# A step-wise softplus, another price for short VectorE instructions, and parameter fetches placed between weight loads

## Chip, cores and metric

The kernel runs on one core of a Trainium2 chip. The metric is the device time of one execution in microseconds (us), as the median over runs; lower is better.

## What is computed

The reference runs two two-layer models one after the other on 256 tokens of width 1024, in float32. A layer of the first kind (called a here) mixes four branches (a state-space scan, two softmax attentions, and an attention on the 64 best keys of an index) with gates and then has a gated feed-forward. A layer of the second kind (b) mixes four other branches (latent attention, spatial gating, gated linear attention, a delta rule), then has a cross attention and a feed-forward. What the change touches in it is softplus, which each kind uses on a few numbers per token:

```python
# layer a, mamba2_branch and fox_branch (log_sigmoid(x) = -softplus(-x))
dt = jax.nn.softplus(dt_raw.astype(jnp.float32) + dt_bias.astype(jnp.float32))   # [1, 256, 8]
log_f = jax.nn.log_sigmoid(f_logit.astype(jnp.float32) + f_bias)                 # [1, 256, 8]
...
# layer b: log_sigmoid of the 128 gate channels of the gated linear attention,
# softplus of 4 step sizes per token of the delta rule
```

and the small parameters of each layer (norm gains, biases, convolution taps, low-rank matrices), which are inputs in HBM.

## The kernel before

**Work.** Layers a0, a1, b0, b1 run in this order. The 256 tokens are two tiles of 128 partitions. All large products are TensorE matmuls on float32 data: each weight chunk (128 partitions x 1024 words, 512 KB) is loaded by one DMA into one of 4 `raw` slots, ScalarE (ACT) copies it rounded to fp32r ("hi", method `high`), VectorE (DVE) writes the remainder ("lo", method `low`), and three fp32r matmuls (hi x hi, hi x lo, lo x hi) make one float32 product (`mm3`). So each chunk costs one long ACT and one long DVE instruction, and TensorE (PE) can use it only after both. Up to 5 chunks are prepared ahead (`LOOK`).

**Order.** The whole program is laid out at build time: one stream of instructions for each engine, executed in order. The layout comes from a planner: a model of the engines' clocks (`Model`, with instruction prices from `Engine.cost`) is advanced as instructions are written down. The main line writes the large matmuls; after each group of them it calls `tick`. `tick` steps side work, which is held as Python generators: `spawn`ed ones, and four *lanes* that carry the branches. A lane is stepped from one `yield` to the next, at most once per tick, only if the model says that its last results are ready by PE's clock, and not while the model has DVE or ACT more than `BACKLOG` = 2750 ns ahead of PE (`behind`). `advance`, called by most ticks, writes `low` and `high` for the coming chunks. When the main line needs the result of a branch that is not finished, `drain` steps the lanes until it is. The plan is made twice; the second pass knows when each chunk falls due.

**Softplus.** `softplus` writes |x| and exp(-|x|) on ACT, then `log1p` writes 14 DVE instructions (an addition, a reciprocal, a series of odd powers in `scalar_tensor_tensor` steps), then one more on DVE. For n = 256 columns (lane C in layers b, `gla`) it yields three times on its way. For n = 32 (lane B in layers a, `small`) and n = 8 (lane B in layers b, `dn`, the delta rule) all of it is written without a yield, so it stands in one piece in DVE's stream. In `dn` two more short instructions stand before it and one behind.

**Prices.** For DVE `Engine.cost` takes (columns + 66)/0.96 ns, or (columns/2 + 66)/0.96 ns for a copy or tensor-scalar instruction outside PSUM, plus 61 ns for each per-partition scalar operand.

**Fetches.** All DMAs are issued by SyncE's queue (SP), in program order, by `Kern.dma`; SP waits in front of each for the buffer to be free. In the feed-forward of each layer but the last, after the first two blocks, `early` allocates and fetches what the next layer needs: constants when the kind changes (`load_consts`, `load_b`; a1 only), and its parameters (`params`): 3 DMAs for a layer a, 8 for a layer b, one behind the other.

Of the kernel before, what the change touches and what calls it, by code (L numbers as in the profile page):

```python
# [165 lines left out]
class Arena:  # L166
# [3 lines left out]
    def __init__(self, ap, words, name, aligned=False):  # L170
        self.ap, self.name, self.aligned = ap, name, aligned
        self.free_ = [(0, words, 0)]
        self.clock = 0
        self.live = {}
        self.pressure = None
# [127 lines left out]
def pair(k, tag):  # L303
    return Pair([Mat(k, 4, 256, tag) for _ in range(2)])
# [49 lines left out]
class Engine:  # L354
# [19 lines left out]
    def cost(self, fn, outs, ins, kw):  # L374
        if self.name == "PE":
            if fn == "transpose":
                return 109.0
            rows, m, n = ins[0].shape[0], ins[0].free_size(), ins[1].free_size()
            if ins[0].dtype == F32R:
                return max(m / 1.2, n / 2.4 + 12) + 1.5  # L380
            if rows <= 64 and m <= 64:
                return 68.0
            share = 0.67 if min(rows, m) <= 64 else 1.0
            return share * 2 * max(m / 1.2 + 1, n / 1.2 + 2)
        n = max(a.free_size() for a in outs[:1] + ins)
        psum = any("PSUM" in str(a.space) for a in ins + outs)
        ptr = sum(1 for a in ins if a.free_size() == 1) if n > 1 else 0
        if self.name == "ACT":
            return (94 if psum else 147) + n / 1.2 + 93 * (ptr + (len(outs) > 1))
        if self.name == "POOL":  # L390
            return 300 + 167 * n if kw.get("op") == OP.pow else 150 + 2.1 * n
        if fn in ("tensor_copy", "tensor_scalar", "memset") and not psum:
            return (n / 2 + 66) / 0.96 + 61 * ptr
        return (n + 66) / 0.96 + 61 * ptr + (1600 * n / 256 if fn == "reciprocal" else 0)


class Kern:
    def __init__(self, tc, dram, layers, tiles, due=None):
        self.tc, self.nc, self.dram, self.layers = tc, tc.nc, dram, layers
        self.due, self.used, self.gemm = due, {}, 0.0  # L400
        nc = self.nc
        self.model = Model()
        self.V, self.A, self.P, self.T = (Engine(e, n, self.model, due is None) for e, n in (
            (nc.vector, "DVE"), (nc.scalar, "ACT"), (nc.gpsimd, "POOL"), (nc.tensor, "PE")))
        wr = NPAIR * 2 * SLOT
        rt, ft, qt, raw, self.junk, banks = tiles
        self.R = Arena(rt[:, wr:], R_ACT, "R", True)
        self.F = Arena(ft, F_WORDS, "F")
        self.Q = Arena(qt, Q_WORDS, "Q")
        self.rawfree = deque(raw[:, i * SLOT:(i + 1) * SLOT] for i in range(NRAW))  # L410
        self.pairfree = deque((rt[:, (2 * i) * SLOT:(2 * i + 1) * SLOT], rt[:, (2 * i + 1) * SLOT:(2 * i + 2) * SLOT])
                              for i in range(NPAIR))
        self.banks = deque(banks)

        self.chunks = []
        self.index = {}
        for layer in layers:
            cbs = plan(layer)
            ch, _ = chunks_of(cbs)
            for name, p, off, nkt, c in ch:  # L420
                self.index[(layer, name, p)] = len(self.chunks)
                self.chunks.append((layer, off, nkt, c))
        self.i_dma = self.i_prep = self.i_done = self.i_cur = 0
        self.raws, self.pairs, self.half = {}, {}, deque()
        self.look = LOOK
        self.lanes = {}
        self.deferred = []
        self.ready, self.mark, self.active, self.pressed = {}, {}, [], 0
        self.keys, self.spawned = {}, 0
        self.gain0 = None  # L430
        self.R.pressure = self.F.pressure = self.Q.pressure = self.relieve


    def dma(self, out, in_):
        if self.due is not None:
            self.nc.sync.dma_start(out, in_)  # L436
        if "SB" in str(out.space):
            self.model.op("DMA", out.nbytes() / 400.0, 2900.0, [out], [])
# [53 lines left out]
    def load(self, most=NRAW):  # L492
        while self.rawfree and self.i_dma < len(self.chunks) and most:
            most -= 1
            layer, off, nkt, c = self.chunks[self.i_dma]
            raw = self.rawfree.popleft()
            src = self.dram["wts_%s%d" % layer][off:off + 128 * nkt * c].rearrange("(p f) -> p f", p=128)
            self.dma(raw[:, :nkt * c], src)
            self.raws[self.i_dma] = raw
            self.i_dma += 1  # L500

    def high(self):

# [327 lines left out]
    def log1p(self, e, out, n):  # L831

        f = self.F.alloc(3 * n, "l1p")
        a, b, c = f.a[:, :n], f.a[:, n:2 * n], f.a[:, 2 * n:3 * n]
        self.ts(a, e, 2.0, OP.add)
        self.V.reciprocal(b, a)
        self.tt(a, e, b, OP.mult)
        if n > 64:
            yield
        self.tt(b, a, a, OP.mult)  # L840
        self.ts(c, b, 1.0 / 17, OP.mult)
        for k in (15, 13, 11, 9, 7, 5, 3):
            if n > 64 and k in (13, 7):
                yield
            self.stt(c, c, 1.0 / k, b, OP.add, OP.mult)
        self.ts(a, a, 2.0, OP.mult)
        self.stt(out, c, 1.0, a, OP.add, OP.mult)
        f.free()

    def softplus(self, x, out, n):  # L850
        f = self.F.alloc(2 * n, "sp")
        a, b = f.a[:, :n], f.a[:, n:2 * n]
        self.act(a, x, AF.Abs)
        self.act(a, a, AF.Exp, scale=-1.0)
        yield from self.log1p(a, b, n)
        self.stt(out, x, 0.0, b, OP.max, OP.add)
        f.free()
# [833 lines left out]
    def layer_b(self, l, hT, nxt, pr, early):  # L1691
# [309 lines left out]
        def dn():  # L2001
# [4 lines left out]
                yield  # L2006
            self.tt(v2(x4), tokv[:, :, 16:20], dtb[:, None, :].to_broadcast([128, 2, 4]), OP.add)
            self.act(v2(be), tokv[:, :, 20:24], AF.Tanh, scale=0.5)
            self.ts(be, be, 1.0, OP.add, 0.5, OP.mult)
            yield from self.softplus(x4, x4, 8)  # L2010
            self.act(ge[:, 0:4], alog, AF.Exp)
# [575 lines left out]
def write(k, layers):  # L2587
    dram = k.dram
    F = k.F
    st = {}  # L2590

    def load_consts(kind):
        if st.get("kind") == kind:
            return
        if "cb" in st:
            st.pop("cb").free()
        st["kind"] = kind
        if kind == "a":
            cb = st["cb"] = F.alloc(NC_A, "ca")
            k.dma(cb.a[:, :NC_A], dram["const_a"])  # L2600
            k.amask, k.mmask, k.tri1 = cb.a[:, 0:384], cb.a[:, 384:768], cb.a[:, 768:1024]
            k.ropec, k.ropes = view(cb.a[:, 1024:1152], 2, 64), view(cb.a[:, 1152:1280], 2, 64)
            k.sel = cb.a[:, 1280:1297]
        else:
            k.load_b(st)

    k.startup(layers[0])
    load_consts(layers[0][0])
    pr = k.params(layers[0])
    hT = pair(k, "hT")  # L2610
    first = k.norm_steps(0, k.x[:, 0], pr["gain"].a, lambda: hT)
    for _ in range(3):
        k.scoped(next, first)
    k.high()
    k.low()
    k.spawn(first, "h0")
    k.flush("h0")

    def second(gain):
        yield from k.norm_steps(1, k.x[:, 1], gain.a, lambda: hT)  # L2620
        gain.free()
    k.spawn(second(pr.pop("gain")), "h1")
    for _ in range(2):
        k.high()
        k.low()
    for i, (kind, l) in enumerate(layers):
        last = i == len(layers) - 1
        nxt_h = {}

        def early(i=i, last=last, nxt_h=nxt_h):  # L2630
            if not last:
                load_consts(layers[i + 1][0])
                nxt_h["p"] = k.params(layers[i + 1])

        def nxt(t, f, i=i, last=last, nxt_h=nxt_h):
            if last:
                yield from k.finish(t, f)
                return
            if t == 0:
                nxt_h["h"] = pair(k, "hT")  # L2640
            yield from k.norm_steps(t, k.x[:, t], nxt_h["p"]["gain"].a, lambda: nxt_h["h"], f)
            if t == 1:
                nxt_h["p"].pop("gain").free()
        if kind == "a":
            k.ffn_a(l, k.layer_a(l, hT, pr), nxt, early)
        else:
            k.layer_b(l, hT, nxt, pr, early)
        if not last:
            k.drain(until=lambda: "h" in nxt_h)
            hT, pr = nxt_h["h"], nxt_h["p"]  # L2650
    k.flush()
    return k.used
# [91 lines left out]
```

## Time and profile before

| | us |
|---|---|
| median of 3 runs (2263.59 to 2268.12) | 2264.24 |
| the profiled execution | 2261.76 |
| its span, first to last instruction | 2259.9 |
| PE busy in the span | 2220.2 (98%) |
| PEld (weight loads, beside PE) busy | 1898.7 (84%) |
| DVE busy | 1535.9 (68%) |
| ACT busy | 1075.5 (48%) |
| POOL (GpSimd) busy | 300.4 (13%) |

A view of the profile is read as follows. Busy times say how much an engine worked, not whether it was waited for; the views of waits and of the order of instructions in time say that. [...] A time in brackets behind an instruction is the idle time of its engine just before it, with what ended it. Instructions of one form that follow one another closely are merged in one row of the order in time (x7: seven of them).

### The profile page before, as it was taken

Reading aid. Unit: us, or ns where it says so; the run is one execution under the profiler, and the core shown is the slowest. Engines: PE = TensorE matmul, PEld = TensorE weight load, DVE = VectorE, ACT = ScalarE, POOL = GpSimd, SP = SyncE. Lnnn points to the kernel's source line nnn. Section 1 sums busy time; section 2 is a strip of 40 time slices with the busy share of each in tenths; the row PEclk is TensorE's granted clock in tenths of the full one; section 3 lists DMA queues with packets and bytes.
Section 4 is the critical chain, followed back from the end, with each engine's and each line's share of the span. In section 5 each row is a group of like instructions: output and inputs, shape, how many; then the busy total and the mean of one; then the engine's idle time right before and its main releaser. Section 6 shows DMA issues by size and latency. Waiting matters only on the chain.

```text
span 2259.9 us, 36096 instructions
## 1 busy us (share of the span) xinstructions
PE 2220.2 (98%) x14196; PEld 1898.7 (84%) x14196; DVE 1535.9 (68%) x2487; ACT 1075.5 (48%) x1699; POOL 300.4 (13%) x266
## 2 busy tenths in 40 slices
PE   8999999999999999999998999999999999999998
PEld 6887788999788788899886788988988677898897
DVE  7887777556888776764777767465566776746554
ACT  4555545444454554543554345444445533545543
POOL 2102110000302120000134220000002432000000
PEclk9999999999999999999998999999999899999999
DMA  6444665655444566565433265456553434544563
GB/s 220 150 133 144 202 227 183 209 176 174 149 131 141 163 202 219 202 215 187 151 105 122 95 206 182 142 176 230 181 163 113 139 112 161 187 159 158 188 210 106
DMA packets 108950, 379.37 MB, mean 168 GB/s; under 512 B 12730, under 2 KB 13164, under 8 KB 108780
## 3 DMA queue, kind: packets, MB, share of 16 engines
q1 hardware_dynamic: 108780, 377.07, 51.0%
q8 instruction: 111, 1.82, 0.3%
q14 instruction: 59, 0.48, 0.1%
HBM read 375.97 MB, written 1.05 MB: 167 GB/s over the span
## 4 chain that ended last, share of the span: by engine, by line
PE 87%; DVE 6%; POOL 2%; issue 2%; ACT 1%; DMA 1%; SPq 0%; POOLq 0%; DVEq 0%; ACTq 0%
PE bank L364 87%; DVE ft L364 4%; DVE rt L364 2%; POOL ft L364 2%; ACT ft L364 1%; DMA raw<-in_wts_a 1%; ACT rt L364 0%; DMA ft<-in_positions 0%; DMA raw<-in_wts_b 0%; ACT junk L364 0%; DVE qt L364 0%; ACT L364 0%; SPq L436 0%; POOLq L2739 0%; POOLq L364 0%
## 5 line engine op out<-in xcount | busy, mean ns | idle before, releaser
L364 PE MATMUL bank<-rt 128*128 128x512 f32 (+3 forms) x10608 | 1975.5, 344 | 13.4 <-DVE rt L364 12.3
L364 PEld LDWEIGHTS bank<-rt 128*128 128x128 f32 x10608 | 1647.7, 190 | 248.0 <-DVE rt L364 18.8
L364 DVE TENSOR_TENSOR rt<-raw,rt 128x1024 fp32r<-128x1024 f32 (+2 forms) x692 | 842.2, 1242 | 266.3 <-ACT rt L364 265.5
L364 ACT ACTIVATE rt<-raw 128x1024 fp32r<-128x1024 f32 (+2 forms) x692 | 693.9, 1034 | 302.1 <-PE bank L364 144.5
L364 POOL TENSOR_TENSOR ft<-ft 128x512 f32<-128x512 f32 (+9 forms) x208 | 247.4, 1200 | 1816.7 <-DVE ft L364 1673.7
L364 PE MATMUL bank<-ft 64*64 64x64 f32 (+13 forms) x3540 | 330.9, 268 | 19.5 <-DVE ft L364 11.8
L364 PEld LDWEIGHTS bank<-ft 64*64 64x64 f32 (+7 forms) x3540 | 254.4, 148 | 102.9 <-issue 35.3
L364 ACT ACTIVATE ft<-bank 128x512 f32<-128x512 f32 (+5 forms) x256 | 135.3, 537 | 334.6 <-PE bank L364 297.8
L364 ACT ACTIVATE ft<-ft 128x128 f32<-128x128 f32 (+7 forms) x238 | 107.6, 463 | 244.0 <-DVE ft L364 228.1
L364 ACT ACTIVATE rt<-bank 128x512 fp32r<-128x512 f32 (+1 forms) x114 | 63.3, 560 | 132.0 <-PE bank L364 131.7
L364 DVE TENSOR_TENSOR ft<-ft 128x512 f32<-128x512 f32 (+5 forms) x122 | 69.2, 568 | 74.2 <-ACT ft L364 71.9
L364 DVE SCALAR_TENSOR_TENSOR ft<-ft 128x512 f32<-128x512 f32 (+5 forms) x211 | 94.3, 467 | 35.1 <-ACT junk L364 16.2
L364 DVE TENSOR_TENSOR ft<-bank,ft 128x512 f32<-128x512 f32 (+8 forms) x160 | 74.1, 491 | 44.6 <-PE bank L364 31.0
L364 DVE SCALAR_TENSOR_TENSOR ft<-ft,bank 128x512 f32<-128x512 f32 (+1 forms) x110 | 70.8, 644 | 35.3 <-PE bank L364 25.7
L364 DVE TENSOR_TENSOR ft<-ft,bank 64x512 f32<-64x512 f32 (+3 forms) x88 | 56.6, 644 | 43.0 <-PE bank L364 39.8
L364 DVE SCALAR_TENSOR_TENSOR ft<-bank,ft 128x256 f32<-128x256 f32 (+5 forms) x124 | 60.4, 509 | 24.7 <-PE bank L364 9.3
L364 DVE TENSOR_SCALAR ft<-ft 128x256 f32<-128x256 f32 (+7 forms) x230 | 58.4, 297 | 26.0 <-ACT ft L364 10.4
L364 DVE COPY ft<-bank 128x384 f32<-128x384 f32 (+5 forms) x96 | 49.3, 541 | 28.5 <-PE bank L364 25.4
L364 ACT ACTIVATE junk<-ft 128x512 bf16<-128x512 f32 (+1 forms) x46 | 27.2, 592 | 64.4 <-DVE ft L364 61.6
L364 POOL TENSOR_SCALAR qt<-qt,ft 64x256 fp32r<-64x256 f32 (+1 forms) x32 | 37.2, 1164 | 131.5 <-PE bank L364 130.6
L364 DVE SCALAR_TENSOR_TENSOR rt<-bank,rt 128x512 fp32r<-128x512 f32 (+1 forms) x72 | 43.3, 612 | 16.5 <-ACT rt L364 16.2
L364 ACT ACTIVATE rt<-ft 128x512 fp32r<-128x512 f32 x46 | 29.0, 630 | 48.7 <-DVE ft L364 47.0
(37 smaller groups left out, 311.2 us busy)
## 6 DMA issues: line engine op xcount, KB each, us to landing
raw<-in_wts_a SPq DMA_DIRECT2D x340, 512.0 KB, 4.2
raw<-in_wts_b SPq DMA_DIRECT2D x312, 512.0 KB, 4.3
raw<-in_wts_b SPq DMA_DIRECT2D x24, 256.0 KB, 2.6
ft<-in_b_gate SPq DMA_DIRECT2D x16, 256.0 KB, 4.5
raw<-in_wts_b SPq DMA_DIRECT2D x8, 440.0 KB, 4.2
raw<-in_wts_a SPq DMA_DIRECT2D x8, 340.0 KB, 4.6
ft<-in_mem SPq DMA_DIRECT2D x4, 512.0 KB, 7.3
ft<-in_x SPq DMA_DIRECT2D x2, 512.0 KB, 3.7
```

What stands on the lines that cost most here:

```text
L364: r = None if self.dry else f(*args, **kw)
```

## The change

Three edits. First, a DVE instruction of at most 64 columns, other than a reciprocal, is priced at 185 ns plus 61 ns for each per-partition scalar. Second, `log1p` yields at its three places whatever n is, `softplus` yields between its ACT part and `log1p`, and `dn` yields between its tanh on ACT and the DVE instruction that reads it. No instruction is added or left out by these yields. Third, while `early` runs `params`, `dma` only notes the fetches; after each weight chunk that `load` issues, one noted fetch is issued. `fetch_all` issues what is left when the next layer's norm begins. Buffers are allocated where they were.

```diff
@@ Engine.cost (DVE)
+        if n <= 64 and fn != "reciprocal":
+            return 185.0 + 61 * ptr
         if fn in ("tensor_copy", "tensor_scalar", "memset") and not psum:
             return (n / 2 + 66) / 0.96 + 61 * ptr
         return (n + 66) / 0.96 + 61 * ptr + (1600 * n / 256 if fn == "reciprocal" else 0)
@@ Kern.__init__
+        self.pend, self.holding = deque(), False
@@ Kern.dma
     def dma(self, out, in_):
+        if self.holding:
+            self.pend.append((out, in_))
+            return
         if self.due is not None:
             self.nc.sync.dma_start(out, in_)
@@ Kern.load (in its loop over free raw slots)
             self.i_dma += 1
+            if self.pend:
+                self.dma(*self.pend.popleft())
+
+    def fetch_all(self):
+        while self.pend:
+            self.dma(*self.pend.popleft())
@@ log1p
         self.tt(a, e, b, OP.mult)
-        if n > 64:
-            yield
+        yield
         self.tt(b, a, a, OP.mult)
         self.ts(c, b, 1.0 / 17, OP.mult)
         for k in (15, 13, 11, 9, 7, 5, 3):
-            if n > 64 and k in (13, 7):
+            if k in (13, 7):
                 yield
             self.stt(c, c, 1.0 / k, b, OP.add, OP.mult)
@@ softplus
         self.act(a, a, AF.Exp, scale=-1.0)
+        yield
         yield from self.log1p(a, b, n)
@@ dn (layer_b)
             self.act(v2(be), tokv[:, :, 20:24], AF.Tanh, scale=0.5)
+            yield
             self.ts(be, be, 1.0, OP.add, 0.5, OP.mult)
             yield from self.softplus(x4, x4, 8)
@@ write: early
                 load_consts(layers[i + 1][0])
+                k.holding = True
                 nxt_h["p"] = k.params(layers[i + 1])
+                k.holding = False
@@ write: nxt
             if t == 0:
+                k.fetch_all()
                 nxt_h["h"] = pair(k, "hT")
```

## Rows read from the trace of the kernel before

**Rows 1.** The page: TensorE's busy time, and its granted clock in 40 slices.

```profile
PE 2220.2 (98%) x14196; PEld 1898.7 (84%) x14196; DVE 1535.9 (68%) x2487; ACT 1075.5 (48%) x1699; POOL 300.4 (13%) x266
...
PEclk9999999999999999999998999999999899999999
```

**Rows 2.** Busy time by stretch: stretch, length, engines (instructions), clock, DMA share, GB/s.

```profile
0.00:50.00 50.00, 38.74 (x182) 31.19 (x183) 36.27 (x75) 23.76 (x35) 12.50 (x16) 1.00 0.65 227
...
1170.00:1240.00 70.00, 59.55 (x551) 49.36 (x551) 51.89 (x106) 34.07 (x72) 36.41 (x33) 0.88 0.39 125
1240.00:1750.00 510.00, 509.98 (x3417) 441.06 (x3418) 322.91 (x451) 239.48 (x363) 53.07 (x50) 1.00 0.50 165
1750.00:1800.00 50.00, 44.84 (x291) 34.03 (x290) 34.52 (x74) 28.39 (x57) 22.16 (x20) 0.86 0.45 137
...
2250.00:2260.00 10.00, 3.03 (x14) 2.18 (x12) 2.45 (x5) 1.45 (x3) 0.55 (x1) 0.78 0.14 52
```

**Rows 3.** Waits of TensorE over the span: releaser, us in total, times, longest.

```profile
PE bank L364 <- DVE rt L364: 12.3, 12, 4.9
PE bank L364 <- DVE ft L364: 11.8, 6, 7.5
PE bank L364 <- POOL ft L364: 7.5, 9, 2.3
```

**Rows 4.** Order in time at the start of layer b0: start, us, instruction, [idle before].

```profile
1187.35 1.31 DVE L364 TENSOR_SCALAR ft<-ft 128x8 f32<-128x8 f32 x2 [1.46 <-ACT ft L364]
...
1189.54 1.37 DVE L364 SCALAR_TENSOR_TENSOR ft<-ft 128x8 f32<-128x8 f32 x7
...
1191.58 2.23 DVE L364 TENSOR_TENSOR rt<-raw,rt 128x512 fp32r<-128x512 f32 x2
...
1192.32 0.80 PE L364 MATMUL bank<-rt 128*128 128x256 f32 x2 [4.91 <-DVE rt L364]
...
1194.85 4.70 PE L364 MATMUL bank<-ft 128*4 128x128 f32 x20
```

**Rows 5.** Busy time in stretches of 2 us, layers b0 and b1.

```profile
1190.00:1192.00 2.00, 0.00 (x0) 0.00 (x0) 1.69 (x10) 0.88 (x1) 0.27 (x1) 0.64 0.00 0
...
1774.00:1776.00 2.00, 2.00 (x12) 1.78 (x11) 1.88 (x4) 0.00 (x0) 0.00 (x0) 0.56 0.38 70
```

**Rows 6.** Order in time at the start of layer b1.

```profile
1771.15 0.30 PE L364 MATMUL bank<-ft 128*128 128x128 f32 x1 [0.86 <-DVE ft L364]
1771.81 4.30 PE L364 MATMUL bank<-ft 128*128 128x128 f32 x25 [0.36 <-DVE ft L364]
...
1790.54 0.42 DVE L364 SCALAR_TENSOR_TENSOR rt<-bank,rt 128x256 fp32r<-128x256 f32 x1
...
1791.01 0.99 PE L364 MATMUL bank<-rt 128*128 128x512 f32 x2 [2.01 <-DVE rt L364]
```

**Rows 7.** Order in time at the starts of layers a0 and a1.

```profile
42.07 0.66 PE L364 MATMUL bank<-ft 128*128 128x128 f32 x4 [1.28 <-POOL ft L364]
...
590.58 1.28 DVE L364 TENSOR_TENSOR ft<-bank,ft 128x512 f32<-128x512 f32 x2
...
594.17 0.66 PE L364 MATMUL bank<-ft 128*128 128x128 f32 x4 [2.28 <-POOL ft L364]
```

**Rows 8.** DVE instructions by form: busy us, mean ns, idle before.

```profile
L364 DVE SCALAR_TENSOR_TENSOR ft<-ft 128x32 f32<-128x32 f32 x25 | 4.8, 192 | 0.9
...
L364 DVE SCALAR_TENSOR_TENSOR ft<-ft 128x8 f32<-128x8 f32 x20 | 3.3, 167 | 0.8
```

**Rows 9.** Order in time around the fetches for layer b0, in layer a1.

```profile
948.45 0.17 DVE L364 CAST ft<-ft 128x2 f32<-128x2 int32 x1 [5.67 <-DMA ft<-in_positions]
...
953.92 0.33 SPq L436 DMA_DIRECT2D ft<-in_sgw  x1
...
955.71 34.30 SPq L436 DMA_DIRECT2D raw<-in_wts_a  x16
...
960.67 0.98 PE L364 MATMUL bank<-rt 128*128 128x256 f32 x6 [0.67 <-DVE rt L364]
```

## Prediction

> **What bounds the kernel now.** I read the page first. PE is busy for 2220.2 of 2259.9 us [rows 1], so 39.7 us is all that waiting costs, and no edit here takes a matmul away. Next come the stretches: from 1240 to 1750 us PE lacks 0.02 us [rows 2], and it is as full in most other places. The 39.7 us sit in a few: 11.3 in the first 50 us, 10.5 at the start of b0 (1170 to 1240), 5.2 at the start of b1 (1750 to 1800), 7.0 at the very end [rows 2], the rest mainly at the start of a1 and in the feed-forward of a1. The first load and the last store make most of the first and all of the last. The same two stretches of layers b also show a granted clock of 0.88 and 0.86 [rows 2], the slices marked 8 on the page [rows 1]. [...] So what can be won is these waits and part of what the low clock costs. The waits of PE name DVE and POOL as releasers [rows 3], at these places.
>
> **Edit 1, the yields.** In b0 DVE stands from 1187.35 to 1191.6 in the softplus of `dn`: after 1.46 us of waiting for ACT come 17 instructions on 8 columns, and only then the "lo" of a weight chunk [rows 4]. PE has waited 4.91 us for it [rows 4], and the granted clock falls to 0.50 within that wait (0.64 over 1190 to 1192) [rows 5]. With the yields the wait for tanh and the 17 instructions are written in six pieces over at least as many ticks, the longest of some seven instructions; at 167 ns [rows 8] that is 1.2 us. A "lo" can be written between any two, since the planner's `advance` comes between ticks. DVE is busy 51.89 of 70 us here [rows 2], so there is room, but not much: the stretch is full of other lanes' work. Terms, in us won:
> - The wait of 4.91: bounds 0 and 4.9. I take 4.5, since the cause stands right in front of the late instruction.
> - What follows: DVE as releaser of PE has 11.8 us in 6 waits, of which 7.5 is the first load [rows 3]; the other five are 4.3, of which b1's two (next but one) are 1.2. The rest is 3.1, most of it in b0 after the narrow matmuls of `dn`, whose result DVE waits for in order. Bounds 0 and 3.1, taken 1.0.
> - The clock in b0: PE is busy 85% of the stretch, so 14.3 of the 16.8 us; the 20 narrow matmuls take 4.70 us there [rows 4] and a like group of 25 takes 4.30 us in b1, mostly at the full clock [rows 6], so they hardly depend on it. The other 9.6 us would be 4.8 shorter. Bounds 0 and 4.8, taken 2.0, because of b1 (next).
> - b1: the same burst, with three short waits behind it. The two at 1771 (0.86 and 0.36) wait for DVE work that was queued behind the burst [rows 6]: bounds 0 and 1.2, taken 0.7. The wait of 2.01 at 1791 is for the last split of the gating branch (1790.54) [rows 6], whose chain runs over POOL and may come earlier or later: bounds -2.9 (three ticks later, at 0.98 us for a group of six matmuls [rows 9]) and 2, taken 0.5. The clock fell in 1774 to 1776, where PE shows no idle time at all, during the narrow matmuls of `dn` [rows 5, 6]. These stay. Of its 14 us, 90% busy, less 1.1 us of narrow ones, half is 5.7: bounds 0 and 5.7, taken 0.8.
> - a0 and a1: there the softplus has 32 columns at 192 ns [rows 8], 15 instructions, and behind it on DVE stands the rotation of queries (590.58), then POOL, then transposes that PE has reached too early by 2.28 us; in a0 by 1.28 us [rows 7]. Some of that is POOL's own time, which stays. Bounds 0 and 2.28, 0 and 1.28; taken 1.2 and 0.5.
>
> What hides the yields themselves is that `dn` and `small` are not waited for soon. Each yield costs its lane at least a tick, some 6 matmuls; if a branch is then late at its projection, `drain` runs its rest with PE idle (third rival).
>
> [...] In b0 the clock fell inside an empty stretch, in b1 in a stretch in which PE counts as busy throughout [rows 5]. [...]
>
> **Edit 2, the price.** Before, 8 columns are priced at 77 ns where rows show 167, and 32 columns at 102 where they show 192 [rows 8]; 185 is closer. No instruction changes by it. It moves the model's DVE clock by 17 x 0.11 = 1.8 us per softplus of `dn`, which places transposes and "lo" better, and keeps lanes back at the 2.75 us gate. I cost it at nothing by itself; it is part of the terms above, and of the third rival.
>
> **Edit 3, the fetches.** 19 parameter DMAs (3, 8 and 8) move behind as many chunk loads in SP's queue. For a1 and b1 no wait of PE stands near them, and the stretch from 1240 to 1750, in which b1's are fetched, is full [rows 2]: nothing is won there, and the cover is the chunks prepared ahead. For b0, in a1's feed-forward, SP stands until 953.92 in front of a parameter and starts weights again at 955.71; PE then waits 0.67 us [rows 9]. But DVE was itself held for 5.67 us for the positions and then by their table [rows 9], and these fetches are not moved. Raw slots come free only by DVE's "lo", so SP's wait was mostly covered by that one. Afterwards each chunk shares the engines with one parameter, where before the last three parameters went ahead of the first chunk. Bounds -1.3 and 1.3, twice that wait, taken 0.3.
>
> **Sum.** 4.5 + 1.0 + 2.0 + 0.7 + 0.5 + 0.8 + 1.2 + 0.5 + 0.3 = 11.5 us. The profiled execution took 2261.76, which would give 2250.3; the median of the runs is 2.5 above it, so 2264.24 - 11.5 = 2253 on the scale of the medians. All upper bounds together are 26.6, that is 2238.
>
> **Rivals.**
> - *The clock falls anyway.* b0's narrow matmuls bring it down as b1's did, a little later, and stay at the low level as long. Then 2.0 and 0.8 are lost from the sum: 8.7 won, 2255.5. For it: the row of b1 [rows 5]; against it: b0's other narrow work is mixed with full matmuls.
> - *Other work takes the place of the burst.* The stretch holds 51.89 us of DVE work in 70 [rows 2]; the lanes that were kept back step in where the burst was, or the pieces are written by a `drain` without a "lo" between them. Then the wait and the fall move but stay: 2264, within 3 us. Against it: the wait is for one chunk whose "lo" needed under a us.
> - *A branch comes late (slower).* The gating branch of b1 is already 2.01 us late at its projection [rows 6]. Higher prices raise the modelled backlog, and more lanes want their turn; if it loses three ticks, PE waits 2.9 us more, and a second full fall of the clock as in b1 (10 us at half, 90% busy) costs 4.5. That is 7.4 us on top: 2272 if b0 gives nothing. It decides from the point where these 7.4 exceed what b0's wait returns, so only with that wait moved rather than gone.
>
> **How the numbers follow.** The forecast has 0.48, the clock falling anyway 0.20, other work in its place 0.18, a late branch 0.14. A measurement of this kernel can tell about 0.2% (4.5 us) from no change. The first two give faster, 0.66 with the part of the second that falls short; the third and that rest give same, 0.20; the fourth slower, 0.14. The range reaches down by most of the clock's bounds, to 2241, and up past the third rival to 2268, leaving about 0.1 on each side.
>
> **What would show it.** Right: no wait of PE over 2 us between 1170 and 1210, "lo" instructions standing between short ones of 8 columns, a granted clock over 0.93 in that stretch, POOL as releaser of PE with under 6 us in total. Wrong: a wait of PE of several us moved to the first gates of b0 or b1; a clock of 0.88 there with no long wait (first rival); new waits before a projection (third rival); waits on weight DMAs after 940 us (edit 3).

## Result and the profile after

The changed kernel takes 2236.93 us (2234.68 to 2239.54, four runs) where the kernel before took 2263.91 on the same chip: 27.0 us less, ratio 0.9878 (95% interval 0.9859 to 0.9897). The forecast was 2253.0, the range 2241 to 2268: the sign was right, the gain 2.3 times what I gave it, and the range missed it. The profiled execution took 2239.54 us, with a span of 2237.8.

The page of the kernel after, to be read against [rows 1]:

```profile
PE 2212.2 (99%) x14196; PEld 1893.0 (85%) x14196; DVE 1536.3 (69%) x2487; ACT 1075.8 (48%) x1699; POOL 288.9 (13%) x266
...
PEclk9999999999999999999999999999999999999999
```

PE has the same 14196 matmuls and is busy 8.0 us less, and its idle time went from 39.7 to 25.6 us, 14.1 less: together the 22.1 us by which the spans differ. Both 8s are gone from the row of the clock. PEclk is the clock granted to TensorE, in tenths of its full speed; in the stretches it is a share of it, and a value between 0.50 and 1.00 is a mixture over the stretch.

The stretches, to be read against [rows 2] (b1 comes some 11 us earlier now); columns as there:

```profile
0.00:50.00 50.00, 41.02 (x191) 33.62 (x191) 37.35 (x72) 25.59 (x36) 10.74 (x13) 0.97 0.71 248
1170.00:1240.00 70.00, 66.79 (x592) 53.53 (x592) 53.89 (x112) 39.61 (x78) 31.51 (x33) 0.93 0.46 151
1240.00:1740.00 500.00, 499.28 (x3362) 431.71 (x3360) 318.95 (x449) 231.61 (x350) 53.00 (x48) 1.00 0.50 164
1740.00:1790.00 50.00, 48.30 (x391) 39.05 (x392) 40.48 (x79) 33.76 (x66) 24.62 (x23) 1.00 0.61 190
```

In b0 PE now lacks 3.2 us of 70 (10.5 before), in b1 1.7 of 50 (5.2 before), and in b1 the clock stays at 1.00. In the first 50 us the clock is 0.97, where it was 1.00.

The waits of PE, against [rows 3]:

```profile
PE bank L364 <- DVE ft L364: 8.1, 3, 7.5
PE bank L364 <- POOL ft L364: 6.3, 9, 1.4
PE bank L364 <- ACT rt L364: 1.5, 3, 1.0
PE bank L364 <- DVE rt L364: 1.1, 3, 0.8
```

DVE's rounded tiles (`rt`, mostly the "lo" of chunks) as releaser went from 12.3 to 1.1 us. The 7.5 is the first load. Behind it POOL is the largest that is left, in waits of at most 1.4 us; `rt` tiles of ACT and DVE come to 2.6 us together.

The order in time at the start of b0, DVE and PE, against [rows 4]:

```profile
1185.45 0.48 DVE L364 TENSOR_SCALAR ft<-ft 128x8 f32<-128x8 f32 x1
1185.93 1.52 DVE L364 TENSOR_TENSOR rt<-raw,rt 128x1024 fp32r<-128x1024 f32 x1
...
1195.61 1.63 DVE L364 SCALAR_TENSOR_TENSOR ft<-ft 128x8 f32<-128x8 f32 x4
1197.15 1.22 DVE L364 TENSOR_TENSOR rt<-raw,rt 128x1024 fp32r<-128x1024 f32 x1
1198.29 0.56 DVE L364 SCALAR_TENSOR_TENSOR ft<-ft 128x8 f32<-128x8 f32 x3
...
1186.41 0.48 PE L364 MATMUL bank<-ft 32*64 32x64 f32 x16 [1.16 <-POOL ft L364]
...
1196.46 0.48 PE L364 MATMUL bank<-ft 32*64 32x64 f32 x16 [1.41 <-POOL ft L364]
...
1201.81 2.66 PE L364 MATMUL bank<-ft 128*4 128x128 f32 x20
```

The burst of 17 is spread over some 14 us, with "lo" instructions between its pieces, and PE waits for POOL twice, 2.6 us in all. The 20 narrow matmuls that took 4.70 us take 2.66.

To place the gain I set the starts of the n-th fp32r matmul of both traces side by side (10608 in each) and read the lead in stretches where only full weight products run. It is 3.9 us after the starts of a0 and a1, 4.6 after the feed-forward of a1 (where b0's parameters are fetched), 11.4 after b0, 22.2 after b1. By stage:

| stage | forecast | profiled pair |
|---|---|---|
| starts of a0 and a1 | 1.7 | 3.9 |
| feed-forward of a1 (fetches) | 0.3 | 0.7 |
| b0 | 7.5 | 6.8 |
| b1 | 2.0 | 10.9 |
| sum | 11.5 | 22.3 |

The other 4.8 us of the median gain are scatter between executions: the profiled execution after is 2.6 above its median, that of before 2.2 below its own.

### The profile page after: what moved, and what is told of

It reads as the page before. It is cut to its first block, busy times and chain, and to the rows that moved or that the text cites. A ratio compares the mean times of both kernels' runs of the same rounds, so it can differ in the third digit from the quotient of the medians.

```text
span 2237.8 us, 36078 instructions
## 1 busy us (share of the span) xinstructions
PE 2212.2 (99%) x14196; PEld 1893.0 (85%) x14196; DVE 1536.3 (69%) x2487; ACT 1075.8 (48%) x1699; POOL 288.9 (13%) x266
## 4 chain that ended last, share of the span: by engine, by line
PE 88%; DVE 7%; issue 1%; ACT 1%; DMA 1%; POOL 1%; SPq 0%; POOLq 0%; DVEq 0%; ACTq 0%
PE bank L364 88%; DVE ft L364 4%; DVE rt L364 3%; DMA raw<-in_wts_a 1%; POOL ft L364 1%; ACT rt L364 1%; ACT ft L364 0%; ACT junk L364 0%; SPq L442 0%; DVE junk L364 0%; POOLq L2755 0%; DVEq L364 0%; POOLq L364 0%; ACTq L364 0%
## 5 line engine op out<-in xcount | busy, mean ns | idle before, releaser
L364 POOL TENSOR_TENSOR ft<-ft 128x512 f32<-128x512 f32 (+10 forms) x208 | 240.5, 1166 | 1808.6 <-DVE ft L364 1563.3
L364 PE MATMUL bank<-ft 64*64 64x64 f32 (+11 forms) x3540 | 324.0, 265 | 15.1 <-DVE ft L364 8.1
```

What stands on the lines that cost most here:

```text
L364: r = None if self.dry else f(*args, **kw)
```

## Experiments

Theory A: the gain comes from cutting the burst of short instructions in front of a "lo", and the price only has to be near the truth for that. Its rival B: any new plan moves this kernel by tens of us, and this one is lucky. Later two further ones: the price acts through the times at which the planner takes results to be ready (R), or through its gate of 2750 ns (G). All runs, each beside runs of the kernel before on the same chip:

| run | what it is | us | before | ratio, interval |
|---|---|---|---|---|
| e1_yields | yields only | 2275.63 | 2263.61 | 1.0048 [1.0033, 1.0063] |
| e2_price | price only | 2263.32 | 2263.61 | 0.9995 [0.9984, 1.0005] |
| e3_yields_price | both, old fetches | 2241.12 | 2263.61 | 0.9894 [0.9878, 0.9911] |
| e4_fetch | fetches only | 2263.98 | 2263.61 | 0.9999 [0.9988, 1.001] |
| e5_noburst | before, burst left out | 2256.6 | 2263.94 | 0.9969 [0.9956, 0.9982] |
| e6_no8 | after, no 8-column yields | 2249.8 | 2263.94 | 0.9937 [0.9922, 0.9951] |
| e7_price150 | after, 150 ns | 2237.46 | 2263.94 | 0.9881 [0.9865, 0.9898] |
| e8_price220 | after, 220 ns | 2236.85 | 2263.94 | 0.9879 [0.9865, 0.9894] |
| e9_price110 | after, 110 ns | 2246.21 | 2266.82 | 0.9907 [0.9892, 0.9922] |
| e10_yields_gate2250 | e1, gate 2250 | 2260.63 | 2266.82 | 0.9975 [0.9965, 0.9986] |
| e11_yields_gate1750 | e1, gate 1750 | 2268.99 | 2266.82 | 1.0011 [1.0002, 1.002] |
| e12_after_gate4000 | after, gate 4000 | 2254.01 | 2266.82 | 0.9943 [0.9923, 0.9963] |
| f1_price_in_readiness | price in readiness only | 2237.82 | 2265.43 | 0.9883 [0.9868, 0.9898] |
| f2_price_in_gate | price in the gate only | 2250.57 | 2265.43 | 0.9947 [0.993, 0.9964] |
| f3_no32 | after, no 32-column yields | 2238.97 | 2265.43 | 0.9889 [0.9874, 0.9904] |
| f4_before_gate2250 | before, gate 2250 | 2259.89 | 2265.43 | 0.9979 [0.9969, 0.9988] |
| f5_yields_fetch | after, old price | 2275.51 | 2264.62 | 1.0052 [1.0036, 1.0067] |
| f6_after_gate2250 | after, gate 2250 | 2232.98 | 2264.62 | 0.9858 [0.9842, 0.9873] |

Us won by stage against the profiled execution of before, from the same matmuls (single executions):

| run | a0, a1 | fetches | b0 | b1 |
|---|---|---|---|---|
| after | 3.9 | 0.7 | 6.8 | 10.9 |
| e1_yields | -3.9 | 0.0 | -3.9 | -7.5 |
| e2_price | 3.3 | -4.8 | 3.2 | -3.3 |
| e3_yields_price | 4.8 | -4.7 | 8.2 | 9.6 |
| e5_noburst | -0.3 | -0.2 | 6.3 | 0.1 |
| e6_no8 | 4.7 | 0.2 | 8.5 | -1.8 |
| e7_price150 | 0.8 | 1.5 | 12.1 | 9.2 |
| e8_price220 | 3.0 | 1.6 | 10.9 | 9.3 |
| f2_price_in_gate | -2.8 | 0.2 | 9.6 | 7.7 |
| f6_after_gate2250 | 6.0 | 0.3 | 13.1 | 10.4 |

**The three edits apart.** The yields alone (the price's two lines and the holding of fetches taken out):

```diff
-        if n <= 64 and fn != "reciprocal":
-            return 185.0 + 61 * ptr
-                k.holding = True
-                k.holding = False
```

> The yields alone, old price, old fetches. If the burst of short instructions is the cause, nearly all of the gain is here: 2238 to 2248 against 2264, no wait of TensorE over 2 us at the start of b0, granted clock at least 0.99 in the mean. If the gain comes from the whole plan being laid out by better prices, this gives 5 us at most: 2259 or more.

Measured 2275.63: 12 us slower. The burst is cut and its wait is gone, but in both layers b a later wait stands in its place. PE and POOL in b0, then PE in b1:

```profile
1264.36 3.31 PE L364 MATMUL bank<-ft 64*64 64x64 f32 x32 [4.55 <-POOL ft L364]
...
1260.39 3.91 POOL L364 TENSOR_TENSOR ft<-ft 128x128 f32<-128x128 f32 x4 [1.49 <-ACT ft L364]
...
1841.42 3.30 PE L364 MATMUL bank<-ft 64*64 64x64 f32 x32 [4.57 <-POOL ft L364]
```

A product of the delta rule (`dn`) stands on PE before its operand can be there, behind four POOL instructions in one piece (two of 128x128, then two of 128x512; the merged row shows the form of its first). The clock falls behind the wait: it is 0.50 from 1264.3 to 1277.9, and the 32 narrow matmuls take 3.31 us where those of the changed kernel take 1.90 at the full clock:

```profile
1243.78 1.90 PE L364 MATMUL bank<-ft 64*64 64x64 f32 x32 [0.52 <-POOL ft L364]
```

This comes near my third rival, a branch that comes late, in size (2272). The kind is another: what is late is a step inside a branch, and not the gating branch at its projection.

The price alone (no new yields, old fetches):

```diff
+        if n <= 64 and fn != "reciprocal":
+            return 185.0 + 61 * ptr
```

> The price alone: the burst stays in one piece. If the burst is the cause, 2256 to 2264, with a wait of TensorE of some 4 us behind the 17 short instructions of b0 and the clock falling as before. If the price is the cause, 2238 to 2248 and no such wait.

Measured 2263.32, no difference. The burst and its wait stand as before, and in a1's feed-forward PE meets a new one (DVE, then PE at both places):

```profile
1189.57 1.37 DVE L364 SCALAR_TENSOR_TENSOR ft<-ft 128x8 f32<-128x8 f32 x7
...
1192.35 0.80 PE L364 MATMUL bank<-rt 128*128 128x256 f32 x2 [4.46 <-DVE rt L364]
...
962.02 4.19 PE L364 MATMUL bank<-rt 128*128 128x256 f32 x16 [2.20 <-ACT rt L364]
```

What it wins at the start of a1 and in b0 it gives back there and in b1. Yields and price together, with the old fetches, and the fetches alone:

```diff
# e3, on after
-                k.holding = True
-                k.holding = False
# e4, on after
-        if n <= 64 and fn != "reciprocal":
-            return 185.0 + 61 * ptr
# and log1p, softplus and dn as before
```

> Yields and price, old fetches; the streams of TensorE, VectorE, ScalarE and GpSimd are those of the changed kernel, only SyncE's order differs. If the fetches are worth nothing: within 2 us of the changed kernel, 2235 to 2239. If they carry part of the gain, as much slower than that: 2242 or more.

> The fetches alone: SyncE's order is the only one that differs from the kernel before. My forecast of this edit: 0.3 us won, between 1.3 lost and 1.3 won, so 2262 to 2265. If spreading the fetches matters, 2258 or less, with the first wait after the fetches of b0 gone; if parameters in front of chunks make weights late, 2267 or more with waits of ScalarE on weight DMAs.

Measured 2241.12 and 2263.98. So the fetches are worth nothing on the old plan and some 4 us on the new one: 4.2 by the medians, 3.6 by the ratios, whose intervals overlap, and 5.4 by the stages of the two traces. The 2241.12 lies between the two cases that were expected. Around them, first with the old fetches (e3), SP's queue in order of time:

```profile
949.06 0.33 SPq L438 DMA_DIRECT2D ft<-in_norm_mix  x1
...
952.28 0.39 SPq L438 DMA_DIRECT2D ft<-in_gw  x1
953.30 8.04 SPq L438 DMA_DIRECT2D raw<-in_wts_a  x5
```

and the stretches there:

```profile
950.00:960.00 10.00, 7.28 (x38) 5.76 (x37) 6.35 (x8) 5.72 (x7) 0.00 (x0) 1.00 1.02 343
960.00:970.00 10.00, 9.47 (x56) 9.27 (x56) 5.88 (x5) 4.23 (x4) 0.00 (x0) 0.66 0.89 314
```

The same two views of the changed kernel, SP's queue:

```profile
951.07 0.33 SPq L442 DMA_DIRECT2D raw<-in_wts_a  x1
951.44 0.43 SPq L442 DMA_DIRECT2D ft<-in_norm_mix  x1
```

and the stretches:

```profile
950.00:960.00 10.00, 8.98 (x51) 7.50 (x50) 7.66 (x9) 6.98 (x8) 0.00 (x0) 1.00 0.67 214
960.00:970.00 10.00, 10.00 (x78) 9.68 (x77) 6.48 (x6) 4.72 (x5) 0.00 (x0) 1.00 1.02 393
```

With eight parameters ahead of the weights PE lacks 3.2 us in 20 and the clock falls to 0.66 in the second ten; with one weight chunk ahead of each parameter it lacks 1.0 and the clock holds.

**Is the burst the cause?** It is left out of the kernel before, and only its yields out of the kernel after:

```diff
# e5, on before
-            yield from self.softplus(x4, x4, 8)
+            self.ts(x4, x4, 0.0, OP.max, 0.5, OP.add)
# e6, on after: each new yield of log1p and softplus only if n != 8, none in dn
-        yield
+        if n != 8:
+            yield
```

> The kernel before, old price, no new yields, old fetches; of the two b layers' token steps the softplus of 8 columns alone is replaced by one short instruction (max with 0, plus 0.5), so this part of the computation is left out and the time is read for that. Theory A (the burst of short 8-column instructions is what makes TensorE wait 4.91 us at 1192 us and the clock fall behind it, and the b layers are worth some 18 us of the 27): no wait over 2 us between 1170 and 1210 us, granted clock over 0.93 there, time about 2245 us, at least 12 us under before. Theory B (the gain is a new order of the whole plan, and the burst was only one of the places where it could show): other work ends up in the burst's place, a wait of several us is found elsewhere in the b layers, and the time stays within 2258 to 2272 us.

> The changed kernel without the yields in the 8-column softplus of the b layers (the one behind the tanh too); the price, the 32-column yields and the fetches stay. Theory A (the b layers' share, some 18 us of the gain, comes from cutting that burst): the burst stands again as in the run with the price alone, TensorE waits 4 to 5 us there, half-clock time of 15 to 25 us, time about 2255 us. Theory B (the plan that price and fetches give is good by itself): within 5 us of the changed kernel, 2235 to 2242 us.

e5 took 2256.6, between the two theories. PE's longer waits in it, the last in b1:

```profile
1177.59 0.60 PE L364 MATMUL bank<-rt 128*128 128x256 f32 x2 [1.56 <-DVE rt L364]
...
1191.54 0.98 PE L364 MATMUL bank<-rt 128*128 128x256 f32 x6 [1.51 <-DVE rt L364]
...
1201.56 0.56 PE L364 MATMUL bank<-ft 128*128 128x128 f32 x2 [3.16 <-DVE ft L364]
...
1798.05 0.48 PE L364 MATMUL bank<-ft 32*64 32x64 f32 x16 [2.15 <-POOL ft L364]
```

The 4.91 is gone and a wait of 1.51 stands in its place. The other two in b0 are old ones, of 1.54 at 1177.11 and 2.51 at 1204.38 in the kernel before. b0 wins 6.3 us, b1 nothing. So on the old plan the burst explains b0 and not b1. e6 took 2249.8, nearer to A (2255) than to B; its loss is all in b1, where the burst stands whole again. DVE and PE there:

```profile
1749.85 1.37 DVE L364 SCALAR_TENSOR_TENSOR ft<-ft 128x8 f32<-128x8 f32 x7
...
1751.89 2.23 DVE L364 TENSOR_TENSOR rt<-raw,rt 128x512 fp32r<-128x512 f32 x2
...
1752.63 0.79 PE L364 MATMUL bank<-rt 128*128 128x256 f32 x2 [5.77 <-DVE rt L364]
...
1755.15 4.70 PE L364 MATMUL bank<-ft 128*4 128x128 f32 x20
```

This is [rows 4] over again, one layer later. In b0 the same burst stands in e6 too, and PE waits 0.74 us (at 1187.02) for the "lo" behind it. So what the burst cost in e6, 0.74 us in b0 and 5.77 in b1, hung on how soon PE needed the "lo" behind it.

**Lucky price or true price?**

```diff
-            return 185.0 + 61 * ptr
+            return 150.0 + 61 * ptr        # e7; 220.0 in e8, 110.0 in e9
```

> The changed kernel with 150 ns in the place of 185 ns as the planner's price of a short DVE instruction (61 ns for a per-partition operand stays). Theory A (the yields need a planner that is near DVE's true time, and 150 ns still is: the profile has 167 to 192 ns): within 6 us of the changed kernel, 2232 to 2243 us, and no wait over 2 us in the b layers. Theory B (each price draws another plan, and 185 ns drew a lucky one): 2250 to 2275 us, with new waits of 3 to 5 us at other places than in the kernel before.

> The changed kernel with 220 ns in the place of 185 ns as the planner's price of a short DVE instruction. Theory A (a planner near DVE's true time is enough): within 6 us of the changed kernel, 2232 to 2243 us. Theory B (a lucky plan): 2250 to 2275 us, with new waits of 3 to 5 us at places where the changed kernel has none.

> The changed kernel with a price of 110 ns for a short DVE instruction, between the old 73 to 77 ns and the 167 to 192 ns that the trace shows for 8 and 32 columns. Theory A (the yields pay as far as the planner's price is near DVE's true time, by degrees): between the changed kernel and the run with the yields alone, 2240 to 2262 us. Theory B (the old price with the yields is one unlucky plan, and any other price undoes it): 2233 to 2243 us.

2237.46, 2236.85 and 2246.21: with the 2236.93 of 185 ns and the 2275.51 of the old price (f5, below) the time falls as the price rises towards the truth, and is flat from 150 ns on. e3, e7 and e8 lie within 4.3 us of the changed kernel and win 9.2 to 9.6 us in b1. Those of e7 and e8 are other plans than its own: DVE's instructions differ from the changed kernel's at 782 and 1032 of 2487 places. Rival B falls for the price. What true is, [rows 8] show for `scalar_tensor_tensor`: 167 ns at 8 columns and 192 ns at 32.

**By which way the price acts.** First by the gate:

```diff
-BACKLOG = 2750.0
+BACKLOG = 2250.0      # e10, on the yields alone; 1750.0 in e11; 4000.0 on after in e12
```

> The yields alone at the old price (2275.6 us in its own run), with one number more changed: the planner lets another lane step only while its clocks for DVE and ACT are at most 2250 ns ahead of that for TensorE, in the place of 2750 ns. Theory A (the price acts through this gate: with prices too low the planner's DVE looks idle, steps are let through too early and pile up in front of what TensorE needs, so a tighter gate makes up for a part of the price): 2245 to 2262 us. Theory B (one unlucky plan, any disturbance moves it): no order between the gates, 2240 to 2275 us. Theory C (the price does not act through the gate, and the yields at the old price are bad in any plan): 2270 us or more.

> As before, with the gate at 1750 ns, some 1000 ns tighter than at first, about what ten short instructions are priced too low (10 x some 95 ns). Theory A (the price acts through the gate): 2232 to 2248 us, near the changed kernel, and below the run with 2250 ns. Theory B (one unlucky plan): 2240 to 2275 us in no order with the run at 2250 ns. Theory C (bad in any plan at the old price): 2270 us or more, with waits of 4 to 5 us for POOL in both b layers.

> The changed kernel (price, yields, fetches) with the gate at 4000 ns in the place of 2750 ns. Theory A (the right price pays because it shuts this gate in time): 2260 to 2280 us, with the waits of the run with the yields alone. Theory B and C (the gate is not how the price pays: it is the times at which a step is taken to be ready): within 8 us of the changed kernel, 2230 to 2245 us.

2260.63, 2268.99 and 2254.01. By the ratios the gate at 2250 gives back some 16 us of what the yields lost, at 1750 only 8: no order, as B said; e10 alone would fit A too, but A's 2232 to 2248 for e11 is missed. With the gate opened to 4000 the changed kernel loses some 15 us, which is between the theories. So the gate matters, but does not stand in for the price. Then the two ways apart, with two clocks for DVE in the planner:

```diff
-        return max(clk["DVE"], clk["ACT"]) - clk["PE"]
+        return max(self.model.other, clk["ACT"]) - clk["PE"]
-                          or max(self.half[0][1], clk["DVE"]) <= clk["PE"] + idle):
+                          or max(self.half[0][1], self.model.other) <= clk["PE"] + idle):
# model.other: DVE's clock by the old price in f1 (operations by the new), the reverse in f2
```

> The changed kernel, but the planner keeps two clocks for DVE: the times at which results are taken to be ready go by the new price, the gate for other lanes and the room for rounding weights go by the old price. Theory R (the price pays through the times of readiness): within 4 us of the changed kernel, 2232 to 2242 us. Theory G (it pays through the gate): like the yields at the old price, 2260 to 2276 us.

> The mirror image: the gate and the room for rounding go by the new price, the times of readiness by the old one. Theory R: 2255 to 2276 us, with waits of 3 to 5 us in the b layers as in the run with the yields alone. Theory G: 2232 to 2245 us.

f1 took 2237.82, and its instruction streams are the changed kernel's but for a few neighbours that change places: the times of readiness alone give all of the gain. f2 took 2250.57, which neither theory had: the gate alone gives 25 of the 38.6 us between f5 and the changed kernel. Either way tells the planner that DVE will be late; the first is enough. The base for this, and the gate once the price is right:

```diff
# f5: after without the two price lines
# f6: after
-BACKLOG = 2750.0
+BACKLOG = 2250.0
```

> The changed kernel without the new price: yields and new fetches at the old price. The yields alone took 2275.6 us, and the fetches made nothing of the kernel before and 4 us of the changed one. If the fetches help any plan with early yields: 2270 to 2273 us; if they help only where the second a layer's rounding is short ahead of them: 2274 to 2277 us. Either way the gate's share of the price is then 20 to 26 us of a possible 33 to 39, and readiness alone gives all.

> The changed kernel with the gate at 2250 ns in the place of 2750 ns. If a tighter gate helps by itself, as it did in the kernel before (4 us): 2231 to 2235 us, the best so far. If it only stood in for a price that was too low, there is nothing left for it: 2235 to 2245 us.

f5: 2275.51, as slow as the yields alone, so the fetches need the price too. f6: 2232.98 (2231.99 to 2233.54), the best time of all, all four runs below the four of the changed kernel; the intervals of the two ratios overlap, though, so its 4 us are likely and not settled.

**The a layers, and how far any plan scatters.**

```diff
# f3, on after: as e6, with 32 in the place of 8, and dn's yield kept
# f4, on before
-BACKLOG = 2750.0
+BACKLOG = 2250.0
```

> The changed kernel without the yields in the 32-column softplus of the two a layers; the 8-column yields, the price and the fetches stay. By the stages of the two traces the a layers' starts give 4 us of the changed kernel's gain, but the price alone already moved the second one's start by 2 us: 2238 to 2242 us if the yields there do the rest; 2235 to 2238 us if the price does it all; above 2250 us if the b layers' gain hangs on the plan of the a layers ahead of them.

> The kernel before with the gate at 2250 ns in the place of 2750 ns, nothing else: how far another plan of the same work moves the time. If such plans scatter little: 2259 to 2269 us. If any new plan can move the kernel as much as the change did: 2240 to 2255 us, or over 2275 us.

2238.97 and 2259.89. The 32-column yields are worth some 2 us, which the overlap of the two intervals leaves unsettled; the price alone already wins 3.3 at the starts of the a layers. Another plan of the old kernel moved it by 5.5 us (0.2%), a fifth of what the change did. With the yields, plans scatter more: the gate alone moved the kernel with the yields only by 15 us (e1, e10, e11) and the changed kernel by 21 (f6, e12). So rival B is answered for prices from 150 to 220 ns at the gate of 2750, and not for every plan.

## Why the prediction was wrong

**Right: where, and b0.** The time that could be won was in the places named [rows 2]. In b0 the steps were right in kind: the wait of 4.91 left, "lo" stands between short instructions, no wait over 2 us is left from 1170 to 1210, and the clock there is 0.96. That 6.8 came out so near the 7.5 forecast is partly luck, since the split was otherwise. The waits gave 6.5 where I took 5.5 (10.47 to 3.93, from 1170 to the start of b1), and the clock some 1.3 where I took 2.0; about 1 us was lost again in small amounts that no view names. The 16.8 and 14 us at the low clock from which I started are 0.12 of 70 and 0.14 of 50 us [rows 2], times two for a clock of 0.50; the profile shows 17.0 us at 0.50 in b0 (the first line here) and 13.7 in b1. For the clock in b0 I had reckoned with 14.3 us of work at 0.50, from the share of the whole stretch. It was 12.8, since two waits lie in the slow time, and after the change it is 10.2: the 3.40 of the second line here and 6.8 behind 1232.9 (last section).

```profile
1190.60:1207.60 17.00, 12.77 (x79) 10.60 (x80) 9.96 (x25) 5.79 (x12) 6.59 (x5) 0.50 0.31 94
...
1205.60:1209.00 3.40, 3.40 (x13) 2.81 (x12) 1.44 (x4) 3.15 (x8) 1.19 (x3) 0.50 0.03 13
```

The second line is my first rival in part: the clock fell 1.1 us behind the narrow matmuls of `dn` (1201.81), 9 us after PE's last wait, but it came back after 3.4 us.

**Wrong: b1, 2.0 against 10.9.** This is the term that broke the forecast, and in it the clock above all, 0.8 taken and 6.8 measured. I left the clock of b1 at 0.8 because it had fallen in a stretch that counts as busy [rows 5], and blamed the narrow matmuls of `dn`, which stay. In the profiled execution after, the clock holds through them:

```profile
1769.76 2.66 PE L364 MATMUL bank<-ft 128*4 128x128 f32 x20
```

The place was not wrong, though. In e3, whose instruction streams on PE, DVE, ACT and POOL are the changed kernel's but for two neighbours on ACT, the clock falls right behind them, for 3.4 us:

```profile
1772.87 2.66 PE L364 MATMUL bank<-ft 128*4 128x128 f32 x20
...
1776.20:1779.60 3.40, 3.40 (x27) 2.50 (x25) 1.90 (x6) 1.55 (x5) 0.00 (x0) 0.50 0.61 204
```

Of the 19 traces that come to these matmuls of b1 at the full clock, it falls in 12 during them or within 1.5 us of their end (the kernel before, e1 to e5, e8 to e10, f3, f4 and f6). So that it did not fall at all in the profiled execution is partly luck. What I had wrong is that the fall would stay as long as it was. What else had differed was ahead of it. The stretches up to the fall (at 1774), in the kernel before:

```profile
1750.00:1760.00 10.00, 9.25 (x67) 8.35 (x66) 5.15 (x6) 8.19 (x18) 5.37 (x4) 1.00 0.65 211
1760.00:1770.00 10.00, 8.82 (x52) 5.56 (x53) 9.10 (x22) 8.09 (x19) 5.57 (x4) 1.00 0.67 211
1770.00:1780.00 10.00, 8.78 (x60) 7.10 (x57) 8.87 (x23) 1.84 (x5) 1.92 (x3) 0.71 0.26 66
```

and the same work in the changed kernel:

```profile
1740.00:1750.00 10.00, 9.38 (x112) 8.36 (x113) 6.59 (x12) 8.82 (x23) 5.49 (x7) 1.00 0.46 140
1750.00:1760.00 10.00, 9.81 (x69) 8.00 (x68) 9.65 (x15) 8.58 (x18) 5.88 (x7) 1.00 0.77 239
1760.00:1770.00 10.00, 10.00 (x59) 7.62 (x57) 9.62 (x24) 4.77 (x10) 2.91 (x3) 1.00 0.70 214
```

PE lacked 3.2 us of these 30 in small waits before, now 0.8; DVE, which had stood half empty in the first row, is busy 25.9 in the place of 23.1. Small waits that I had priced one by one, at 0.7 and 0.5, were also what stood ahead of the fall. In sum b1's waits gave 3.5 (5.16 to 1.70). The low clock gave 6.8: PE had been busy all through its 13.7 us, 10.3 of them here and 3.4 from 1791.3.

```profile
1774.20:1784.50 10.30, 10.30 (x53) 8.08 (x52) 6.09 (x15) 2.94 (x9) 1.34 (x3) 0.50 0.35 103
```

Together that is 10.3 of the 10.9. My upper bound for the clock of b1, 5.7, was nearer to this 6.8 than the 0.8 that I took; I had let the row of b1 [rows 5] hold me to the lower one.

The other runs fit the account. From 1700 to 1900 us, nine traces lack 1.2 to 3.6 us of PE and have 0 to 6.8 us at the clock of 0.50 (the changed kernel, e3, e7 to e9, f1 to f3 and f6). The other eleven lack 5.2 to 8.9 us and have 10.2 to 23.9. That fewer waits are the cause of the shorter fall is still argued from these rows; no run here changed the waits of b1 and nothing else.

**Wrong: narrow matmuls do not depend on the clock.** I compared the 20 narrow matmuls of b0 (4.70 us) with a row of 25 in b1 (4.30), "mostly at the full clock" [rows 4, 6]. But a merged row shows the form of its first instruction alone. Taken by form, that row is five products of 128x128 and the same 20 narrow ones (eight more of 128x4 and eight of 128x2 beside these):

```profile
L364 PE MATMUL bank<-ft 128*128 128x128 f32 x5 | 0.9, 295 | 0.4 <-DVE ft L364 0.4
L364 PE MATMUL bank<-ft 128*4 128x128 f32 x4 | 0.8, 272 | 0.0
```

And the clock fell at 1774.2, in the middle of the 20. They take 4.70 us at the low and 2.66 at the full clock. To read a merged row as one form at one clock was the mistake.

**Wrong: the price costs and gives nothing by itself.** Alone it does give nothing (e2). But I credited the b terms to the yields, and the yields without it lose 11 to 12 us (e1, f5). What the price changes is the planner's belief of when results are ready (f1), and I had put it down as a side effect that places work "better". With the old price the kernel would have come out slower, near the time of the third rival.

**Mis-sized: the rest.** The starts of the a layers gave 3.9 against 1.7, and more by the price (3.3 in e2, some 2 in f3) than by the yields as I had it. Edit 3 gave some 4 us on the new plan (e3), outside my bounds of 1.3, which I took from the old plan. There weight loads start again at 955.71 [rows 9]; in e3 they do so at 953.30, which is 2.4 us later for PE, since e3 is 4.8 us ahead by then, and ACT waits 3.4 us for a chunk. Of the signs named, POOL as releaser came to 6.3, just over the 6 set. After 940 us ACT waits longer for weights (6.4 us from 940 to 970, 3.2 before), but PE does not (0.9 us, 1.5 before).

That plans with both yields and a near price are that good in b1, while neither gives it alone, is shown as a fact (e3, e7, e8 and f6 against e1, e2, e5 and e6). A gate of 4000 takes it away again (e12: PE lacks 8.9 us there, with 13.7 at the clock of 0.50). Which of the many instructions that change places carries it stays open.

## What to carry to other kernels

Where a planner lays out the order of instructions, cutting a lump of work into steps and pricing those steps truly are one edit: the finer the steps, the more the plan rests on the prices, so read the measured time per instruction off the trace first. A lump of short instructions cost here what PE had to wait for the next long one behind it (4.91 us in b0 of the kernel before, 0.74 and 5.77 in b0 and b1 of e6), so look which result the busy engine needs next. When small waits stand ahead of a fall of the clock, price them with the fall: in b1 some 3 us fewer waits went with 5 to 7 us less lost to the clock (the changed kernel, e3, e7, e8, f3, f6).

## What the runs showed of the hardware

TensorE's clock also fell with no wait at all. In the profiled execution after it went from 1.00 to 0.50 at 1232.9, in b0:

```profile
1230.00:1232.00 2.00, 2.00 (x44) 1.50 (x40) 1.02 (x3) 0.00 (x0) 2.00 (x3) 1.00 0.69 234
1232.00:1234.00 2.00, 2.00 (x9) 1.18 (x6) 0.88 (x3) 1.41 (x2) 0.02 (x1) 0.72 0.15 61
1234.00:1236.00 2.00, 2.00 (x40) 1.82 (x41) 0.50 (x2) 0.77 (x2) 0.00 (x0) 0.50 0.00 0
```

PE counts 2.00 of 2.00 throughout and has no wait from 1200 to this fall, and the work of the ten us ahead was a mixture of full products and 80 narrow ones of 4x64 and 32x64. In f6 PE lacks under 0.1 us in the 30 us ahead of either fall in the b layers (1202.4 and 1762.1), and both start within 1 us of the end of `dn`'s narrow matmuls. In the four runs the mean clock was 0.996, 1.000, 0.997 and 0.999, and the times 2239.54, 2234.68, 2239.08 and 2234.78: the same program, 4.9 us apart. So 0.2% of this kernel hangs on something that its order of instructions does not settle.
